# Early products without GpSimd work, and scale and shift of the second token set on the transposed tiles

## The chip, the cores and the metric

The kernel runs on one core of a Trainium2 chip. Its engines are TensorE (PE in the rows; its weight loads PEld), VectorE (DVE), ScalarE (ACT), GpSimd (POOL) and SyncE (SP), which issues nearly all DMAs. Each engine runs its own instructions strictly in the order in which the program gives them; an instruction waits for semaphores that other engines or DMAs raise. The metric is the device time of one execution in microseconds.

## The reference

Two layers of a diffusion backbone over 768 tokens (256 context, 512 latent) of width 1024. Each layer is a half-step feed-forward block, a token mixer (differential attention in layer 0, neighbourhood attention in layer 1), and a second half-step feed-forward block. Each sub-layer normalises before and after itself, and shift, scale and gate come from a conditioning vector:

```
def _rmsnorm(h, g):
    hf = hf * lax.rsqrt(jnp.mean(hf * hf, axis=-1, keepdims=True) + NORM_EPS)
    return hf.astype(h.dtype) * g

def _ffn_sublayer(h, mod, g_pre, g_post, w_in, w_out):
    shift, scale, gate = mod
    u = _rmsnorm(h, g_pre) * (1 + scale) + shift
    a, b = jnp.split(u @ w_in, 2, axis=-1)
    y = (jax.nn.silu(a) * b) @ w_out
    return h + MACARON_W * gate * _rmsnorm(y, g_post)

for i in range(2):          # mods of x from silu(c), of the context from silu(c_ctx)
    h = _ffn_sublayer(h, mods[0:3], ...)
    h = h + mods[5] * _rmsnorm(mixer(modulate(_rmsnorm(h, g[2]))), g[3])
    h = _ffn_sublayer(h, mods[6:9], ...)     # in the last layer, latent tokens only
```

In the differential attention each head's output is normalised, multiplied by a learned gain of 128 numbers (`da_subln_g`) and by a constant; the kernel folds both into one column, `gsub`.

## The kernel before

**Products.** Every fp32 operand of a matmul is split into a high part (a ScalarE cast to fp32r, `...h`) and a low part (an fp32 subtraction, `...l`), and a product is three matmul passes: hi x hi, lo x hi, hi x lo (`mm3`, line 132; the split's two instructions have lines 126 and 127).

**First gemms.** The four feed-forward blocks are `f00`, `f01` (layer 0), `f10`, `f11` (layer 1); `u @ w_in` of each is a `FirstGemm`. The six token tiles of 128 make two sets, tiles 0 to 2 and 3 to 5 (`f11`: two sets of two latent tiles, 2, 3 and 4, 5). Most of the product is done by a Strassen-like scheme that pairs the two sets (groups "R" and "F": sums of weight quarters times sums of the two sets' `u`). Before these, while the second set's `u` isn't ready, the kernel does the products that need only the first set: the heads, items "E", 7, 7, 6 and 5 of them for `f00`, `f01`, `f10`, `f11`. One E item takes two 128x1024 weight blocks (x = 0 for a, x = 1 for b), splits each (`prep`; with `EPOOL = (1, 1, 0, 1)` the low part of block x = 0 is subtracted by GpSimd in `f00`, `f01` and `f11`; names `f003s0l` = head of f00, item 3, block 0, low), does 4 x 12 matmuls (`early_a`: `e3x`, copied by ScalarE to `e3p`; `early_b`: `e3v`, to which VectorE adds `e3p`, giving `e3s`, line 533), then a SiLU on ScalarE and the product a x b on GpSimd (line 537), which goes to HBM by a DMA (`hr`). PSUM gives the `e..x` and `e..v` products a few banks in turn: a product waits until an older one has been added or copied out.

**The second set beside the heads.** A generator, stepped by `late_step()` between the head's products, makes the second set's `u`: `rest` (residual, line 905; norm), then `u_rows`: scale and shift row-wise, `un = h * rstd * A + B` with A and B as 128x1024 rows (lines 352 and 353 on VectorE; `UCOL` gives the columns of one tile that go to ScalarE and GpSimd instead, lines 347 to 349: 768 of 1024 before `f01`, all before `f10`, 384 before `f11`), then `to_sums`: eight TensorE transposes per tile into a pair of PSUM banks and, from there, eleven VectorE and five ScalarE instructions that form the sums and their splits (lines 312 to 331). In `f00` the modulation is done otherwise: by columns after the transposes (lines 189 to 193), `us` and `ut`.

**Order.** A list scheduler sets the order on each engine when the kernel is built; engines keep it. Around the `f00` head stands the load of `gsub` (line 1058) and its VectorE scaling (line 1059). The modulation rows are computed pairwise in `mods_pairs` (`mb`, `am`, lines 243 to 247), beside the first gemms.

Of the kernel before, what the change touches and what calls it, by code (L numbers as in the profile page):

```python
# [41 lines left out]
EPOOL = (1, 1, 0, 1)  # L42
UCOL = (((0, 0, 0), (0, 0, 0)), ((0, 0, 0), (0, 640, 0)), ((0, 0, 0), (0, 0, 768)), ((0, 0, 0), (0, 1024, 0)), ((0, 0, 0), (0, 640, 0)), ((0, 0, 0), (0, 384, 0)))
# [13 lines left out]
def kernel(  # L57
# [12 lines left out]
    da_subln: bass.AP,  # L70
# [63 lines left out]
    svec = const.tile([P, 5 * KC], F32, name="svec")  # L134
# [3 lines left out]
    ucol = svec[:, 2 * KC :].rearrange("p (m k o) -> p m k o", m=3, o=1)  # L138
# [160 lines left out]
    def to_sums(pool, t, first, un, ps, sums, name):  # L299
# [34 lines left out]
    def u_rows(pool, tiles, hs, uns, rows, pss, name, sums=None, rs=None, split_u=None, by_act=False):  # L334
        rs = rs or []
        n_t = len(tiles)
        for n in range(n_t + 2):
            if n < n_t and len(rs) <= n:
                rs.append(rstd_of(pool, hs[n], uns[n], f"{name}_{tiles[n]}", by_act and n == 2))
            if 0 < n <= n_t:  # L340
                un = uns[n - 1]
                k = kind(tiles[n - 1])
                a, b = rows["A", k], rows["B", k]
                cut = split_u[n - 1] if split_u else 0
                if cut:
                    c = slice(0, cut)
                    nc.scalar.activation(un[:, c], hs[n - 1][:, c], AF.Copy, scale=rs[n - 1])
                    nc.gpsimd.tensor_tensor(out=un[:, c], in0=un[:, c], in1=a[:, c], op=ALU.mult)
                    nc.gpsimd.tensor_tensor(out=un[:, c], in0=un[:, c], in1=b[:, c], op=ALU.add)
# [4 lines left out]
            yield
            if n > 1:
                t = tiles[n - 2]
                if sums:
# [60 lines left out]
    class FirstGemm:  # L418
        def __init__(self, pool, l, j, sets, name, lead=False):
# [1115 lines left out]
```

## Time and profile before

| | |
|---|---|
| time, median of 3 runs | 2891.31 us (2886.37 to 2895.78) |
| the profiled execution | 2882.43 us, span 2880.0 us, mean granted TensorE clock 0.988 |
| TensorE busy | 2755.4 us (96%) |
| VectorE, ScalarE, GpSimd busy | 1986.4 (69%), 1209.5 (42%), 883.0 us (31%) |
| heads on TensorE | f00 32.6 to 122.2 us, f01 1045.2 to 1124.4, f10 1595.7 to 1656.5, f11 2497.7 to 2547.3 |

Rows read as follows. A timeline row has start, duration, engine, line, operation, what it writes and reads with the shape, and in brackets the idle time before it and what ended it. Durations of neighbours overlap a little, since an instruction starts before the one in front has left the engine. A granted clock of 1.00 is 2.4 GHz; an average below it in a window means that part of the window ran at 1.2 GHz.

### The profile page before, as it was taken

How to read it: one execution, taken by the hardware profiler on the slowest of the kernel's cores; microseconds unless marked ns; L12 is line 12 of the kernel's file. 1: busy time of each engine (PE TensorE's matmuls, PEld its weight loads, DVE VectorE, ACT ScalarE, POOL GpSimd, SP SyncE). 2: the span in 40 equal slices, each digit the busy share in tenths (PEclk: the TensorE clock that was granted, in tenths of full speed). 3: DMA queues.
4: the chain of work that ended last, by engine and by line, in shares of the span. 5: the costliest groups of instructions: out<-in, count | busy, mean ns of one | idle time of the engine just before them, and what ended most of it. 6: DMA issues, size and time to landing. Idle time of an engine off the chain costs nothing. (4 is left out here: it accounts for less than half of the span.)

```text
span 2880.0 us, 41455 instructions
## 1 busy us (share of the span) xinstructions
PE 2755.4 (96%) x15928; PEld 2441.6 (85%) x15928; DVE 1986.4 (69%) x2554; ACT 1209.5 (42%) x1894; POOL 883.0 (31%) x715
## 2 busy tenths in 40 slices
PE   7799999999999988999999999999999999889999
PEld 5788998888888778899988888998878888789987
DVE  5677664667777696777555867674654556799965
ACT  5322333435555553233343522233444446544444
POOL 2455420020000055554210455340122110377710
PEclk9999999999999999999999999999999999999999
DMA  8577346643343476853465577436644444654375
GB/s 279 189 278 273 103 147 218 213 123 86 105 118 88 140 240 199 285 172 104 171 210 193 178 271 266 162 107 219 217 160 118 118 118 130 222 167 147 125 252 192
DMA packets 304820, 511.55 MB, mean 178 GB/s; under 512 B 17456, under 2 KB 226224, under 8 KB 297456
## 3 DMA queue, kind: packets, MB, share of 16 engines
q1 hardware_dynamic: 304336, 508.26, 53.7%
q8 instruction: 125, 2.05, 0.3%
q14 instruction: 71, 0.58, 0.1%
q10 hardware_dynamic: 288, 0.66, 0.1%
HBM read 410.15 MB, written 63.05 MB: 164 GB/s over the span
## 5 line engine op out<-in xcount | busy, mean ns | idle before, releaser
L1243 POOL TENSOR_TENSOR bias<-bp,nneg 128x128 f32<-128x128 f32 x112 | 52.3, 505 | 190.1 <-issue 99.2
L127 DVE TENSOR_TENSOR f01hl<-f01h,f01hh 128x384 fp32r<-128x384 f32 x44 | 26.4, 599 | 74.7 <-ACT f01hh L126 74.6
L127 DVE TENSOR_TENSOR f00hl<-f00h,f00hh 128x384 fp32r<-128x384 f32 x44 | 26.5, 602 | 72.9 <-ACT f00hh L126 72.8
L127 DVE TENSOR_TENSOR f10hl<-f10h,f10hh 128x384 fp32r<-128x384 f32 x44 | 26.0, 591 | 67.7 <-ACT f10hh L126 67.6
L243 PE MATMUL am<-aw,s 128*32 128x512 f32 x512 | 68.3, 606 | 4.1 <-DVE f10b0c L548 3.0
L126 ACT CAST f10hh<-f10h 128x384 fp32r<-128x384 f32 x44 | 22.7, 516 | 113.6 <-PE f10y L721 93.9
L126 ACT CAST f01hh<-f01h 128x384 fp32r<-128x384 f32 x44 | 22.7, 516 | 109.8 <-PE f01y L721 95.1
L126 ACT CAST f00hh<-f00h 128x384 fp32r<-128x384 f32 x44 | 22.7, 516 | 107.2 <-PE f00y L721 92.7
L132 PE MATMUL av<-pt,davh 128*128 128x256 f32 x224 | 44.6, 292 | 0.0
L247 DVE TENSOR_TENSOR mb<-am,mb 128x512 f32<-128x512 f32 x64 | 43.7, 683 | 0.0
L1305 PE MATMUL nav<-npt,navh 128*64 128x256 f32 (+1 forms) x320 | 39.3, 365 | 0.0
L132 PEld LDWEIGHTS av<-pt,davh 128*128 128x128 f32 x224 | 36.4, 193 | 1.3 <-ACT pt L1165 0.2
L1305 PEld LDWEIGHTS nav<-npt,navh 128*64 128x64 f32 x320 | 22.0, 136 | 12.2 <-issue 1.9
L132 PE MATMUL av<-pt,davl 128*128 128x256 f32 x112 | 31.7, 283 | 0.0
L126 ACT CAST f11hh<-f11h 128x256 fp32r<-128x256 f32 x44 | 17.7, 406 | 33.1 <-DMA f11h<-hr 22.1
L127 DVE TENSOR_TENSOR f11hl<-f11h,f11hh 128x256 fp32r<-128x256 f32 x44 | 20.2, 464 | 13.4 <-ACT f11hh L126 13.4
L243 PEld LDWEIGHTS am<-aw,s 128*32 128x32 f32 x512 | 10.1, 108 | 20.4 <-issue 10.2
L282 POOL TENSOR_SCALAR f01y0r<-f01y0s 128x1 f32<-128x1 f32 x1 | 0.2, 192 | 84.5 <-ACT f01y0j L276 84.5
L282 POOL TENSOR_SCALAR f10y0r<-f10y0s 128x1 f32<-128x1 f32 x1 | 0.2, 192 | 84.5 <-ACT f10y0j L276 84.5
L282 POOL TENSOR_SCALAR f00y0r<-f00y0s 128x1 f32<-128x1 f32 x1 | 0.2, 192 | 84.5 <-ACT f00y0j L276 84.5
L282 POOL TENSOR_SCALAR f00y3r<-f00y3s 128x1 f32<-128x1 f32 x1 | 0.2, 193 | 79.3 <-ACT f00y3j L276 79.3
L282 POOL TENSOR_SCALAR f10y3r<-f10y3s 128x1 f32<-128x1 f32 x1 | 0.2, 192 | 79.3 <-ACT f10y3j L276 79.3
(9736 smaller groups left out, 11615.4 us busy)
## 6 DMA issues: line engine op xcount, KB each, us to landing
aw<-in_ada_w SPq DMA_DIRECT2D x63, 1024.0 KB
f00r<-in_ffn_w_in SPq DMA_DIRECT2D x22, 1024.0 KB
f01r<-in_ffn_w_in SPq DMA_DIRECT2D x22, 1024.0 KB
f10r<-in_ffn_w_in SPq DMA_DIRECT2D x22, 1024.0 KB
f11r<-in_ffn_w_in SPq DMA_DIRECT2D x22, 1024.0 KB
f00o<-in_ffn_w_out SPq DMA_DIRECT2D x21, 1024.0 KB
f01o<-in_ffn_w_out SPq DMA_DIRECT2D x21, 1024.0 KB
f10o<-in_ffn_w_out SPq DMA_DIRECT2D x21, 1024.0 KB
```

The lines of the kernel that those rows point to most:

```text
L126: nc.scalar.copy(hi, src)
L127: eng.tensor_tensor(out=lo, in0=src, in1=hi.bitcast(F32), op=ALU.subtract)
L132: nc.tensor.matmul(ps, lhsT=lhs[i], rhs=rhs[j], start=first and n == 0, stop=last and n == 2)
L243: nc.tensor.matmul(ps[32 * c : 32 * c + 32], lhsT=s32[:, k], rhs=w[:, c // 2, c % 2 * 512 : c % 2 * 512 + 512], start=True, stop=True,)
L247: nc.vector.tensor_tensor(out=acc, in0=ps, in1=acc, op=ALU.add)
L282: nc.gpsimd.tensor_scalar(r, ss, 1.0, EPS, ALU.mult, ALU.add)
L1243: nc.gpsimd.tensor_tensor(out=bias[:, m, :].rearrange("p (a b) -> p a b", a=8), in0=view, in1=neg[:, m, :].rearrange("p (a b) -> p a b", a ...
L1305: nc.tensor.matmul(av[64 * i : 64 * i + 64, half * 256 + c0 : half * 256 + c0 + n], lhsT=made[u]["v"][0][:, key, vc : vc + 64], rhs=made[u ...
```

## The change

Five things. (1) `EPOOL` is gone: VectorE does every low part of the heads' weight splits (19 subtractions of 128x1024 move: 7 in `f00`, 7 in `f01`, 5 in `f11`). (2) The product a x b of each E item moves from GpSimd to VectorE (25: 7, 7, 6, 5). (3) For the second set before `f01`, `f10` and `f11` ScalarE alone writes `un = h * rstd` (128x1024), and after the eight transposes applies scale and shift in place on the PSUM banks with eight 128x128 activations per tile (3, 3 and 2 tiles: 64 instructions); scale and shift come as columns (`cols`, 128x2x8) by two DMAs of 4-byte elements per group of tokens. (4) `gsub` is a column of the constants loaded at the start and is scaled there. (5) In `mods_pairs` the bias and gain rows of a pair are loaded before its weights. The numbers of `UCOL` that concern (3) go; its two for the inputs of the mixers stay.

```diff
@@ -39,8 +39,7 @@
 PROG0 = "SF1F2b"
 PROG1 = "SF12Fb"
 SUMV = (2, 2, 2, 2)
-EPOOL = (1, 1, 0, 1)
-UCOL = (((0, 0, 0), (0, 0, 0)), ((0, 0, 0), (0, 640, 0)), ((0, 0, 0), (0, 0, 768)), ((0, 0, 0), (0, 1024, 0)), ((0, 0, 0), (0, 640, 0)), ((0, 0, 0), (0, 384, 0)))
+UCOL = {1: (0, 640, 0), 4: (0, 640, 0)}
 EVAC = "AA"
 JUNK = 1
 NEXT = (2, 4)
...
@@ -131,11 +129,12 @@
         for n, (i, j) in enumerate(PASSES):
             nc.tensor.matmul(ps, lhsT=lhs[i], rhs=rhs[j], start=first and n == 0, stop=last and n == 2)
 
-    svec = const.tile([P, 5 * KC], F32, name="svec")
+    svec = const.tile([P, 5 * KC + 1], F32, name="svec")
     nc.sync.dma_start(svec, cvec)
     nc.scalar.activation(svec[:, 0 : 2 * KC], svec[:, 0 : 2 * KC], AF.Silu)
     s2 = svec[:, 0 : 2 * KC].rearrange("p (j k) -> p j k", j=2)
-    ucol = svec[:, 2 * KC :].rearrange("p (m k o) -> p m k o", m=3, o=1)
+    ucol = svec[:, 2 * KC : 5 * KC].rearrange("p (m k o) -> p m k o", m=3, o=1)
+    gsub = svec[:, 5 * KC :]
     mcol = const.tile([P, 2, KC, 2], F32, name="mcol")
     s32 = const.tile([P, KC, 32], F32, name="s32")
     nc.vector.memset(s32, 0.0)
@@ -221,7 +220,6 @@
                 return
             pair, k = seq[q]
             nm = f"{pair[0][0]}{pair[0][1]}"
-            ws[q] = pair_loads(pool, pair, k)
             if k == 0:
                 for x, tag in (("b", "mb"), ("g", "araw")):
                     rows[x] = pool.tile([P, 512], F32, tag=tag, name=f"m{x}{nm}")
@@ -229,6 +227,7 @@
                         row = ada_b[l, m * D : (m + 1) * D] if x == "b" else norm_g[l, g_index[m]]
                         src = bass.AP(tensor=row.tensor, offset=row.offset, ap=[[512, 2], [0, 32], [1, 512]])
                         nc.sync.dma_start(rows[x][64 * a : 64 * a + 64, :], src)
+            ws[q] = pair_loads(pool, pair, k)
 
         load(0)
         yield
@@ -296,7 +295,7 @@
             nc.vector.tensor_tensor(out=ulo[cs], in0=tp, in1=uhi[cs].bitcast(F32), op=ALU.subtract)
             yield
 
-    def to_sums(pool, t, first, un, ps, sums, name):
+    def to_sums(pool, t, first, un, ps, sums, name, cols=None):
         tt, sub, add = nc.vector.tensor_tensor, ALU.subtract, ALU.add
         mine = slice(t * P, (t + 1) * P)
         twin = slice(first * P, (first + 1) * P)
@@ -305,6 +304,8 @@
         if un is not None:
             for k in range(KC):
                 nc.tensor.transpose(tp[:, k, :], un[:, k * P : (k + 1) * P], ident)
+            for k in range(KC):
+                nc.scalar.activation(tp[:, k], tp[:, k], AF.Identity, scale=cols[:, 1, k : k + 1], bias=cols[:, 0, k : k + 1])
             yield
         b12, b22 = tp[:, 0:4, :], tp[:, 4:8, :]
         ta = pool.tile([P, 2, 4, P], F32, tag="R1", name=name + "ta")
@@ -340,22 +341,27 @@
             if 0 < n <= n_t:
                 un = uns[n - 1]
                 k = kind(tiles[n - 1])
-                a, b = rows["A", k], rows["B", k]
-                cut = split_u[n - 1] if split_u else 0
-                if cut:
-                    c = slice(0, cut)
-                    nc.scalar.activation(un[:, c], hs[n - 1][:, c], AF.Copy, scale=rs[n - 1])
-                    nc.gpsimd.tensor_tensor(out=un[:, c], in0=un[:, c], in1=a[:, c], op=ALU.mult)
-                    nc.gpsimd.tensor_tensor(out=un[:, c], in0=un[:, c], in1=b[:, c], op=ALU.add)
-                if cut < D:
-                    c = slice(cut, D)
-                    nc.vector.scalar_tensor_tensor(un[:, c], hs[n - 1][:, c], rs[n - 1], a[:, c], ALU.mult, ALU.mult)
-                    nc.vector.tensor_tensor(out=un[:, c], in0=un[:, c], in1=b[:, c], op=ALU.add)
+                if "c" in rows:
+                    nc.scalar.activation(un, hs[n - 1], AF.Copy, scale=rs[n - 1])
+                else:
+                    a, b = rows["A", k], rows["B", k]
+                    cut = split_u[n - 1] if split_u else 0
+                    if cut:
+                        c = slice(0, cut)
+                        nc.scalar.activation(un[:, c], hs[n - 1][:, c], AF.Copy, scale=rs[n - 1])
+                        nc.gpsimd.tensor_tensor(out=un[:, c], in0=un[:, c], in1=a[:, c], op=ALU.mult)
+                        nc.gpsimd.tensor_tensor(out=un[:, c], in0=un[:, c], in1=b[:, c], op=ALU.add)
+                    if cut < D:
+                        c = slice(cut, D)
+                        nc.vector.scalar_tensor_tensor(un[:, c], hs[n - 1][:, c], rs[n - 1], a[:, c], ALU.mult, ALU.mult)
+                        nc.vector.tensor_tensor(out=un[:, c], in0=un[:, c], in1=b[:, c], op=ALU.add)
             yield
             if n > 1:
                 t = tiles[n - 2]
                 if sums:
-                    yield from to_sums(pool, t, t - sums["t2"] + sums["t1"], uns[n - 2], pss[n - 2], sums, f"{name}_{t}")
+                    yield from to_sums(
+                        pool, t, t - sums["t2"] + sums["t1"], uns[n - 2], pss[n - 2], sums, f"{name}_{t}", rows["c"][kind(t)]
+                    )
                 else:
                     yield from to_uT(t, uns[n - 2], pss[n - 2], f"{name}_{t}")
 
@@ -423,7 +429,6 @@
             self.n = len(sets[0]) * P
             self.slot = (2 * l + j) % 2
             early = EARLY[2 * l + j]
-            self.epool = EPOOL[2 * l + j]
             self.items = [("E", g, 0) for g in range(early)]
             for g in range(NF // 2):
                 self.items += [("R" if g < early else "F", g, x) for x in (0, 1)]
@@ -462,7 +467,7 @@
                         if x == 0:
                             o = pool.tile([P, 2, 2, KC, P], F32R, tag="T" + "hl"[g], name=f"{nm}s")
                         dst = [o[:, x, y] for y in range(2)]
-                    ops[x] = split(r[x], [P, KC, P], f"{nm}s{x}", dst, nc.gpsimd if self.epool >> x & 1 else nc.vector)
+                    ops[x] = split(r[x], [P, KC, P], f"{nm}s{x}", dst)
                     yield
                 return
             a12, a21, a22 = r[:, 4:8, 0:P], r[:, 0:4, P:256], r[:, 4:8, P:256]
@@ -534,7 +539,7 @@
                 if x == 0:
                     nc.scalar.activation(sa[0], sa[0], AF.Silu)
                     late_step()
-            nc.gpsimd.tensor_tensor(out=sa[0], in0=sa[0], in1=sa[1], op=ALU.mult)
+            nc.vector.tensor_tensor(out=sa[0], in0=sa[0], in1=sa[1], op=ALU.mult)
             nc.sync.dma_start(hdr[self.slot][2 * g][:, self.t1 * P : self.t1 * P + n], sa[0])
             self.step(i + 1, 9)
             late_step()
@@ -896,8 +901,16 @@
         rs = []
         yns = [x[0] for x in st]
         if nxt is not None:
-            rows_for(pool, nxt[0], nxt[1] + 1, kinds, "A", rows)
-            rows_for(pool, nxt[0], nxt[1], kinds, "B", rows)
+            turn = nxt[1] != 3 and si == 1
+            if turn:
+                rows["c"] = {}
+                for j in kinds:
+                    cols = rows["c"][j] = pool.tile([P, 2, KC], F32, tag=f"cols{j}", name=f"{name}c{j}")
+                    for m in range(2):
+                        nc.sync.dma_start(cols[:, m], mdram[nxt[0]][nxt[1] + m][j].rearrange("(k p) -> p k", p=P))
+            else:
+                rows_for(pool, nxt[0], nxt[1] + 1, kinds, "A", rows)
+                rows_for(pool, nxt[0], nxt[1], kinds, "B", rows)
         for n, t in enumerate(tiles):
             cut = D // 2 if nxt is None and final and n == len(tiles) - 1 else D
             for z in range(0, D, cut):
@@ -917,7 +930,7 @@
             if nxt[1] != 3 and si == 1:
                 sums = more[1] = sums_for(pool, more[0], name, 2 * nxt[0] + nxt[1] // 6)
             pss = [ys[t] for t in tiles] if final else [None] * len(tiles)
-            yield from u_rows(pool, tiles, [hs[t] for t in tiles], yns, rows, pss, name, sums, rs, UCOL[3 * nxt[0] + nxt[1] // 3][si], nxt[1] == 3 and si)
+            yield from u_rows(pool, tiles, [hs[t] for t in tiles], yns, rows, pss, name, sums, rs, UCOL.get(3 * nxt[0] + nxt[1] // 3) if si else None, nxt[1] == 3 and si)
 
     def raw_cols(w, c0, nm):
         r = wraw([P, KC, 256], nm)
@@ -1054,9 +1067,6 @@
         w = da_w_in
         cs = pool.tile([P, 2, NLAT], F32, name="rope", bufs=1)
         nc.sync.dma_start(cs, rope_cs)
-        gsub = const.tile([P, 1], F32, name="gsub")
-        nc.sync.dma_start(gsub, da_subln.rearrange("(p o) -> p o", o=1))
-        nc.vector.tensor_scalar(gsub, gsub, 1.0 - LAM_INIT, None, ALU.mult)
         lv = pool.tile([P, 4, 64], F32, tag="oo", name="lv", bufs=1)
         nc.sync.dma_start(lv, da_lambda.rearrange("a d -> (a d)").partition_broadcast(P).rearrange("p (a d) -> p a d", a=4))
         lp = pool.tile([P, 2, 64], F32, tag="sq", name="lp", bufs=1)
...
@@ -1399,6 +1409,7 @@
         first = FirstGemm(mp, 0, 0, full, "f00", lead=True)
         nc.vector.tensor_scalar(ucol[:, 1], ucol[:, 1], 1.0, None, ALU.add)
         nc.vector.tensor_tensor(out=ucol[:, 1], in0=ucol[:, 1], in1=ucol[:, 2], op=ALU.mult)
+        nc.vector.tensor_scalar(gsub, gsub, 1.0 - LAM_INIT, None, ALU.mult)
         turns = {}
         new_u("in")
 
...
```

VectorE in the `f00` head, before, around the scaling of `gsub` (`us` is tile 5 before its sums, `in_5ta` its first sum, `f004s1l` and `f005s1l` the low parts of weight blocks):

```order
L331 TENSOR_TENSOR inul<-in_4tb,inuh 128x4x128
L533 TENSOR_TENSOR f00e3s_725<-f00e3v_744,f00e3p 128x384
L127 TENSOR_TENSOR f004s1l<-f00r_570,f004s1h 128x1024
L192 TENSOR_TENSOR us_799<-in5T,mcol 128x1024
L1059 TENSOR_SCALAR gsub<-gsub 128x1
L193 TENSOR_TENSOR us_799<-us_799,mcol 128x1024
L313 TENSOR_TENSOR in_5ta<-us_799,inuh 128x512
L327 TENSOR_TENSOR inul<-us_799,inuh 128x4x128
L314 TENSOR_TENSOR in_5ta<-in_5ta,inul 128x512
L324 TENSOR_TENSOR in_5tb<-us_799,in_5tb 128x512
```

and after:

```order
L538 TENSOR_TENSOR f00e3s_726<-f00e3v_745,f00e3p 128x384
L125 TENSOR_TENSOR f004s1l<-f00r_571,f004s1h 128x1024
L542 TENSOR_TENSOR f00e3s_725<-f00e3s_725,f00e3s_726 128x384
L191 TENSOR_TENSOR us_800<-in5T,mcol 128x1024
L125 TENSOR_TENSOR f005s0l<-f00r_674,f005s0h 128x1024
L192 TENSOR_TENSOR us_800<-us_800,mcol 128x1024
L538 TENSOR_TENSOR f00e4s_828<-f00e4v_830,f00e4p 128x384
L314 TENSOR_TENSOR in_5ta<-us_800,inuh 128x512
L328 TENSOR_TENSOR inul<-us_800,inuh 128x4x128
L315 TENSOR_TENSOR in_5ta<-in_5ta,inul 128x512
```

The `gsub` instruction is gone from between the two steps of `us`; the product `f00e3s` x `f00e3s` (line 542) and `f005s0l` have come in.

VectorE at the start of the `f01` head, before (`o0i` is the residual, `o0n` its normalised and modulated rows, tiles 3 to 5 in turn):

```order
L352 SCALAR_TENSOR_TENSOR o0n_9397<-o0i_9345,o_3r,A_07_9218 128x1024
L127 TENSOR_TENSOR f011s1l<-f01r_9354,f011s1h 128x1024
L533 TENSOR_TENSOR f01e0s_9488<-f01e0v_9506,f01e0p 128x384
L353 TENSOR_TENSOR o0n_9397<-o0n_9397,B_06_9222 128x1024
L352 SCALAR_TENSOR_TENSOR o0n_9405<-o0i_9347,o_4r,A_07_9218 128x1024
L352 SCALAR_TENSOR_TENSOR o0n_9413<-o0i_9349,o_5r,A_07_9218 128x256
L353 TENSOR_TENSOR o0n_9405<-o0n_9405,B_06_9222 128x1024
L353 TENSOR_TENSOR o0n_9413<-o0n_9413,B_06_9222 128x256
L313 TENSOR_TENSOR o_3ta<-o0y_8999,o0uh 128x512
L314 TENSOR_TENSOR o_3ta<-o_3ta,o0ul 128x512
L533 TENSOR_TENSOR f01e1s_9585<-f01e1v_9587,f01e1p 128x384
L315 TENSOR_TENSOR o_3ta<-o0y_8999,o_3ta 128x512
```

and after:

```order
L125 TENSOR_TENSOR f011s0l<-f01r_9352,f011s0h 128x1024
L538 TENSOR_TENSOR f01e0s_9488<-f01e0v_9490,f01e0p 128x384
L538 TENSOR_TENSOR f01e0s_9489<-f01e0v_9507,f01e0p 128x384
L125 TENSOR_TENSOR f011s1l<-f01r_9352,f011s1h 128x1024
L542 TENSOR_TENSOR f01e0s_9488<-f01e0s_9488,f01e0s_9489 128x384
L125 TENSOR_TENSOR f012s0l<-f01r_9447,f012s0h 128x1024
L538 TENSOR_TENSOR f01e1s_9592<-f01e1v_9594,f01e1p 128x384
L125 TENSOR_TENSOR f012s1l<-f01r_9447,f012s1h 128x1024
L538 TENSOR_TENSOR f01e1s_9593<-f01e1v_9616,f01e1p 128x384
L542 TENSOR_TENSOR f01e1s_9592<-f01e1s_9592,f01e1s_9593 128x384
L125 TENSOR_TENSOR f013s0l<-f01r_9533,f013s0h 128x1024
L314 TENSOR_TENSOR o_3ta<-o0y_8997,o0uh 128x512
```

The row-wise steps of lines 352 and 353 are gone from in front of the first addition of `f01e1s`; low parts `...s0l` and products of line 542 have come in, and the sums of tile 3 stand behind item 1.

ScalarE at the same place, before:

```order
L126 CAST f012s0h<-f01r_9446 128x1024
L519 COPY f01e1p<-f01e1x_9537 128x384
L347 ACTIVATE o0n_9413<-o0i_9349,o_5r 128x768
L519 COPY f01e1p<-f01e1x_9538 128x384
L312 CAST o0uh<-o0y_8999 128x4x128
L126 CAST f012s1h<-f01r_9446 128x1024
```

and after:

```order
L124 CAST f012s0h<-f01r_9447 128x1024
L308 ACTIVATE o0y_8997<-o0y_8997,o0c_9437 128x128
L345 ACTIVATE o0n_9411<-o0i_9347,o_5r 128x1024
L308 ACTIVATE o0y_8997<-o0y_8997,o0c_9437 128x128
L124 CAST f012s1h<-f01r_9447 128x1024
L308 ACTIVATE o0y_8997<-o0y_8997,o0c_9437 128x128
L540 ACTIVATE f01e1s_9592<-f01e1s_9592 128x384
L308 ACTIVATE o0y_8997<-o0y_8997,o0c_9437 128x128
L124 CAST f013s0h<-f01r_9533 128x1024
L308 ACTIVATE o0y_8997<-o0y_8997,o0c_9437 128x128 x3
L524 COPY f01e2p<-f01e2x_9647 128x384
L308 ACTIVATE o0y_8997<-o0y_8997,o0c_9437 128x128
L313 CAST o0uh<-o0y_8997 128x4x128
```

In front of the first cast of tile 3's sums (line 313; line 312 before) there now stand that tile's eight in-place activations (line 308), and among them a whole-row copy of another tile (line 345), three weight casts, a SiLU and a copy of item 2.

## Rows read from the trace of the kernel before

**Rows 1.** The page, part 1: busy time, share of the span and instructions of each engine.

```profile
PE 2755.4 (96%) x15928; PEld 2441.6 (85%) x15928; DVE 1986.4 (69%) x2554; ACT 1209.5 (42%) x1894; POOL 883.0 (31%) x715
```

**Rows 2.** The waits of TensorE: who, for what; us in total, times, longest.

```profile
PE f01e2x L132 <- DVE f01e1s L533: 5.5, 1, 5.5
PE f00e4v L132 <- ACT f00e4p L519: 5.3, 1, 5.3
PE f01b0W L132 <- DVE mb L247: 5.1, 1, 5.1
PE f11a0X L132 <- ACT f115bh L126: 4.8, 1, 4.8
...
PE f01e5x L132 <- DVE f01e4s L533: 3.7, 2, 3.3
...
PE f00e5x L132 <- ACT f00e5p L519: 3.0, 1, 3.0
...
PE f11e2x L132 <- DVE f11e1s L533: 2.9, 1, 2.9
...
PE f00e4x L132 <- DVE f00e3s L533: 2.6, 1, 2.6
...
PE f00b0W L132 <- DVE mb L247: 2.2, 1, 2.2
```

**Rows 3.** Windows: length, busy (instructions) of each engine, granted clock, DMA share, GB/s.

```profile
53.00:123.00 70.00, 55.88 (x289) 53.32 (x288) 54.66 (x56) 32.15 (x49) 31.98 (x21) 0.90 0.58 179
93.00:110.00 17.00, 12.62 (x39) 11.64 (x40) 15.90 (x14) 6.99 (x12) 11.37 (x6) 0.62 0.32 109
1045.00:1125.00 80.00, 68.14 (x367) 64.81 (x366) 68.78 (x65) 41.42 (x64) 49.32 (x33) 0.94 0.64 199
1595.00:1657.00 62.00, 56.81 (x321) 53.52 (x320) 58.38 (x63) 35.66 (x57) 30.32 (x22) 1.00 0.60 194
2497.00:2548.00 51.00, 37.77 (x266) 35.42 (x267) 46.36 (x46) 27.14 (x45) 32.47 (x22) 0.90 0.56 179
```

**Rows 4.** Timeline of VectorE, 88 to 96 us: start, us, line, operation [idle before].

```profile
91.38 0.15 DVE L1059 TENSOR_SCALAR gsub<-gsub 128x1 f32<-128x1 f32 x1 [5.98 <-DMA gsub<-in_da_subln]
...
93.35 0.69 DVE L327 TENSOR_TENSOR inul<-us,inuh 128x512 fp32r<-128x512 f32 x1
```

**Rows 5.** Timeline of ScalarE, 88 to 96 us.

```profile
92.70 0.62 ACT L312 CAST inuh<-us 128x512 fp32r<-128x512 f32 x1 [9.44 <-DVE us L193]
```

**Rows 6.** Timeline of SyncE's queue, 78 to 92 us.

```profile
80.31 1.09 SPq L1058 DMA_DIRECT2D gsub<-in_da_subln  x1
```

**Rows 7.** Timeline of GpSimd, 53 to 60 us.

```profile
56.43 2.67 POOL L127 TENSOR_TENSOR f003s0l<-f00r,f003s0h 128x1024 fp32r<-128x1024 f32 x1
```

**Rows 8.** Timeline of VectorE, 53 to 123 us.

```profile
57.15 2.50 DVE L327 TENSOR_TENSOR inul<-us,inuh 128x512 fp32r<-128x512 f32 x1 [0.31 <-ACT inuh L312]
...
114.87 1.84 DVE L127 TENSOR_TENSOR f007bl<-f007s,f007bh 128x1024 fp32r<-128x1024 f32 x1 [0.39 <-ACT f007bh L126]
```

**Rows 9.** Timeline of VectorE, 1045 to 1125 us.

```profile
1047.09 3.32 DVE L905 SCALAR_TENSOR_TENSOR o0i<-o0n,o0y3r,o0i 128x1024 f32<-128x1024 f32 x1
...
1063.62 4.78 DVE L353 TENSOR_TENSOR o0n<-o0n,B 128x1024 f32<-128x1024 f32 x2
...
1069.64 0.55 DVE L533 TENSOR_TENSOR f01e1s<-f01e1v,f01e1p 128x384 f32<-128x384 f32 x1
...
1108.35 2.40 DVE L127 TENSOR_TENSOR f017dl<-f01r,f017dh 128x512 fp32r<-128x512 f32 x1
```

**Rows 10.** Groups by line and form, VectorE, 53 to 123 us: busy, mean ns.

```profile
L127 DVE TENSOR_TENSOR f003s1l<-f00r,f003s1h 128x1024 fp32r<-128x1024 f32 x1 | 1.2, 1218 | 0.0
```

**Rows 11.** One line's instructions: ns shortest/median/longest, from and to, shape.

```profile
L537 POOL TENSOR_TENSOR f00e0s<-f00e0s,f00e0s x1: 1007/1007/1007, 52.6 to 52.6; 128x384 f32<-128x384 f32 x1
```

**Rows 12.** The same of another line, on ScalarE.

```profile
L189 ACT ACTIVATE ut<-in2T,mcol x8: 449/458/475, 28.0 to 43.3; 128x128 f32<-128x128 f32 x8
```

**Rows 13.** The same of a third line, on ScalarE.

```profile
L347 ACT ACTIVATE f01n<-f01i,f_4r x1: 1158/1158/1158, 1603.3 to 1603.3; 128x1024 f32<-128x1024 f32 x1
```

More of the change, by code (lines that the diff above doesn't have):

```diff
@@ L69 @@
     da_lambda: bass.AP,
-    da_subln: bass.AP,
     na_w_in: bass.AP,
@@ L1328 @@
         OVER = {
-            "post": (("h", 3), ("yn", 3), ("G0", 1), ("A0", 1), ("B0", 1), ("R1", 2), ("ss", 4), ("rs", 4)),
+            "post": (("h", 3), ("yn", 3), ("G0", 1), ("A0", 1), ("B0", 1), ("R1", 2), ("ss", 4), ("rs", 4), ("cols0", 1)),
             "mid": (("sa", 2), ("c0", 1), ("c1", 1), ("u2", 2), ("aw", 2), ("mb", 2)),
@@ L1487 @@
             np.asarray(a).reshape(-1, P).T
-            for a in (inputs["c"], inputs["c_ctx"], inputs["ada_b"][0, : 2 * D], inputs["norm_g"][0, 0])
+            for a in (inputs["c"], inputs["c_ctx"], inputs["ada_b"][0, : 2 * D], inputs["norm_g"][0, 0], inputs["da_subln_g"][0])
         ],
@@ L1520 @@
         "da_w_in": inputs["da_w_in"][0], "da_w_out": inputs["da_w_out"][0], "da_lambda": inputs["da_lambda"][0],
-        "da_subln": inputs["da_subln_g"][0], "na_w_in": inputs["na_w_in"][0], "na_w_out": inputs["na_w_out"][0],
+        "na_w_in": inputs["na_w_in"][0], "na_w_out": inputs["na_w_out"][0],
         "rpb_pad": runs, "rope_cs": rope, "na_neg": neg,
```

## The prediction

> **What bounds the kernel now.** I read the page's busy shares first: TensorE is busy for 96% of the span [rows 1], so a change to the other engines counts only where TensorE waits for them or runs at a lower clock. The view of TensorE's waits says where [rows 2]: nearly all of its long waits for VectorE and ScalarE lie in the heads (names `e2x`, `e4v`, `e5x`, `a0X`), besides two on the modulation sums (`mb`). The windows give each head a ceiling [rows 3]: TensorE idles 14.1 us of 70 in the later part of the `f00` head (70 less 55.88 busy), 11.9 of 80 in `f01`, 5.2 of 62 in `f10`, 13.2 of 51 in `f11`. There is a second loss: the granted clock is 0.90, 0.94, 1.00 and 0.90, and just 0.62 from 93 to 110 us, behind the 5.3 us wait of `f00e4v`. A mean of 0.62 between the levels 1.2 and 2.4 GHz is 76% of the time at the lower one; 76% of the 12.62 busy us, halved, is 4.8 us lost. VectorE is the fullest of the others there (54.7 of 70, 68.8 of 80, 58.4 of 62, 46.4 of 51).
>
> Two things fill it. One is a stall: VectorE sat 5.98 us at 91.38 for the DMA of `gsub`, which nothing in the head needs, between two steps of tile 5's `us` [rows 4]; ScalarE, in order, stood 9.44 us at the cast of `us` with the copy `f00e4p` behind it [rows 5], and TensorE waited 5.3 us for that copy [rows 2]. The other is a stretch: a subtraction of 128x512 takes 0.69 us [rows 4], but 2.50 at 57.15 [rows 8], inside GpSimd's `f003s0l` (56.43, 2.67 us) [rows 7]. Against the usual duration of their shape, 12 VectorE instructions of the `f00` head (the first at 57.15, the last at 114.87 [rows 8]) are too long by 13.9 us in sum, 15 in the `f01` head (1047.09 to 1108.35 [rows 9]) by 19.3.
>
> **The change part by part.**
> *Work onto VectorE.* A 128x1024 subtraction takes 1.22 us [rows 10], a 128x384 operation 0.55 [rows 9]; less some 0.08 that neighbours overlap, 1.14 and 0.47. `f00` and `f01` get 7 x (1.14 + 0.47) = 11.3 us each, `f10` 6 x 0.47 = 2.8, `f11` 5 x 1.14 and 5 products of two thirds the size, some 7.3. The product itself isn't shown on VectorE; its ends are the addition of the same size (0.55) and GpSimd's 1.01 [rows 11]; I take 0.55, VectorE's own.
>
> *f00.* Freed: 6.0 (`gsub`) + 13.9 (stretch, as GpSimd has no work of size left in the head) - 11.3 = 8.6 us by which VectorE is ahead when it reaches `f005s1l`, for which item 5 waits. Half of the clock's 4.8 comes back, 2.4. The low parts of items 1 and 2 now stand in front of the first set's `inul`, which delays the first products: -1.5 (between 0 and two subtractions, 2.4). Sum +9.5. What is late next is VectorE still, not TensorE.
>
> *f01.* The row-wise steps go: 2.25 tiles of two instructions near 1.2 us, 5.2; their stretch is inside the 19.3 (the pair at 1063.62 took 4.78 [rows 9]). 5.2 + 19.3 - 11.3 = 13.2 us. The first addition of `f01e1s` at 1069.64 [rows 9], for which TensorE waited 5.5 [rows 2], then follows its product at once. But sums now come in whole blocks: tile 3's, eleven instructions of some 0.6 us, stand in front of `f013s1l`, and cannot begin before ScalarE has done three casts and eight activations. From the order and these durations I get waits of some 2.8 us for two of the tiles: 13.2 - 5.6 = +7.6, within the ceiling of 11.9 idle and some 4 of clock.
>
> *f10.* The freed time exceeds what TensorE loses (5.2 idle, clock 1.00 [rows 3]); half of it: +2.6 (0 to 5).
>
> *f11.* Waits of 2.9 (`f11e2x`) and 4.8 (`f11a0X`) hang on the same two causes [rows 2]; with a clock of 0.90 I take +6 (2 to 9); behind the head the groups wait for VectorE anyhow.
>
> *In-place scale and shift.* 64 activations of 128x128. The nearest row is the same operation from PSUM into SBUF, 458 ns [rows 12]; into PSUM it isn't shown. Ends: 128x512 in one cast took 0.62 [rows 5], so 155 ns of pure data each, and 475, the longest [rows 12]. At 458 it is 3.7 us per tile, 29.3 in all, and eight copies of 1.16 [rows 13] less the three that were partly there, some 6 more. ScalarE is busy 41.4 of 80 us, 35.7 of 62 and 27.1 of 51 [rows 3], so 11 to 13 us per head find room: I price them at nothing beyond the 5.6 taken off above. If the room is no cover, they cost up to 35.
>
> *Columns.* Six DMAs in place of the second set's rows. Nearest row: `gsub`, also of 4-byte elements, held SyncE's queue for 1.09 us [rows 6] and its reader stood until 11.1 us after the issue [rows 4, 6]. They are issued among the head's weight loads, well over 11 us before the first activation: 0, at most 6 x 1.09 = 6.5 if the weight loads behind them come late by it.
> The Trainium skill (DMA: Bandwidth & Descriptors, Specifications) puts the smallest transfer at line rate at 512 bytes and says that smaller ones are done as read-modify-write; it speaks against these columns. The 11.1 us of `gsub` agree, though they hold the queue's wait too. By the rule the columns would be priced at their upper end, 6.5, and the forecast would come to 2869.5.
>
> *gsub and the modulation rows.* With its load at the start, `gsub` costs one small VectorE instruction there: 0. The two waits for `mb` (5.1 and 2.2 [rows 2]) came from a low part in front of it on VectorE that waits for a late load; in the new order it stands further behind. A third of 7.3: +2.5 (-1 to 6).
>
> Sum: 9.5 + 7.6 + 2.6 + 6 + 2.5 = 28.2. From the profiled execution's 2882.4 this makes 2854.2. That execution was 8.9 below the median of the runs shown (2891.3); on the median, 2863.
>
> **The stretch, weighed.** All rests on the stretch being GpSimd's doing; what the rows show is overlap in time. The Trainium skill (GPSIMD Engine Reference, Key points) says that GpSimd shares its SBUF interfaces with VectorE, and that instructions with two SBUF inputs contend. By that rule the 33 us go with the moved work; without it they stay, which is the second rival below.
>
> **Rivals.**
> 1. *ScalarE becomes the bound (slower).* In each of the three heads its activations stand among the weight casts and the copies that free PSUM banks. From the point at which its queue is later than TensorE's next product, every added instruction is exposed: 29.3 + 6 = 35.3 against 28.2 gained is +7, and a lower clock behind such waits some 3 more: 2901. Against it: half of ScalarE's time in `f01` is free; for it: it runs in order, and it stood 9.44 us once already. 6%.
> 2. *The stretch stays.* Then `f00` gets 6.0 - 11.3, `f01` 5.2 - 11.3, `f11` 3.9 (1.6 tiles' row-wise steps at 2.4) - 7.3, `f10` 4.8 (two tiles') - 2.8, the modulation 2.5: -10.3, so 2902. Against it: long instructions begin and end with GpSimd's. 4%.
> 3. *Loads and stores pace the heads.* Then only the gsub stall goes: 6.0, 2885. For it: each item needs 1 MB of weights, and a DMA share of 0.64 [rows 3]; against it: TensorE's longest waits there name VectorE and ScalarE. 11%.
> 4. *TensorE runs through.* The waits of all heads go (44.4 us idle in rows 3), about what they hold less the transposes' own gaps: some 42, 2849. It needs a VectorE with room, which the sums above don't leave in `f00`. 8%.
>
> **How the numbers follow.** The forecast, 2863, has 71%, with 2849 to 2878 as its own range from the terms' ends. Rivals 1 and 2 have 10%, 3 has 11%, 4 has 8%. About 0.3% (8.7 us) is what a measurement of this kernel tells from no change: faster is under 2882.6, so 0.71 + 0.08 = 0.79; same 0.11; slower 0.10. The range from 2843 to 2886 takes in rivals 3 and 4 and leaves out the slower ones and a gain above 48.
>
> **What would show it.** Right: no VectorE idle for a DMA near 80 to 92 us, `f00e4v` waiting under 1 us, and a clock near 1.00 where it was 0.62; 128x512 subtractions in the heads at 0.7 us; `f01e2x` waiting under 1 us and waits of 2 to 3 us at `f01e3x` or `f01e4x`; activations of line 308 near 0.46 us. Wrong: ScalarE's activations ending TensorE's waits (rival 1), long VectorE instructions with GpSimd idle (rival 2), DMA as the releaser of head items (rival 3), or VectorE waiting for `cols`.

## The result, and the profile after

The changed kernel takes 2861.0 us (median of 4, 2858.8 to 2862.2) against 2890.1 of the kernel before on the same chip: a ratio of 0.9897, interval 0.9879 to 0.9915, so 25 to 35 us less. The forecast was 2863. Between the two profiled executions the spans differ by less, 2880.0 to 2859.1: that of before was one of its fastest (2882.4, where its median over 17 runs is 2889.9), that of after stands at its median. What follows by stages adds up to these 20.9 us.

The page's busy shares after answer to [rows 1]: GpSimd is 100 us less busy, and VectorE 33, though it took over GpSimd's work in the heads.

```profile
PE 2749.9 (96%) x15928; PEld 2438.5 (85%) x15928; DVE 1953.7 (68%) x2584; ACT 1237.4 (43%) x1963; POOL 783.3 (27%) x665
```

TensorE's waits after, to be read beside [rows 2] (who, for what; us in total, times, longest):

```profile
PE f00e4v L130 <- DVE f00e3s L538: 6.2, 1, 6.2
PE f01e3x L130 <- DVE f01e2s L538: 5.5, 1, 5.5
...
PE f00e5x L130 <- ACT f00e5p L524: 3.9, 1, 3.9
...
PE f11e3x L130 <- ACT f11e3p L524: 3.0, 1, 3.0
PE f01e5x L130 <- DVE f01e4s L538: 3.0, 1, 3.0
...
PE f10e4v L130 <- DVE f10e3s L538: 2.0, 1, 2.0
```

Gone are the waits for `mb` at `f01b0W` and `f00b0W` (5.1 and 2.2) and that of `f11a0X`; that of `f01e2x` has shrunk to 0.9. But `f00e4v` waits longer than before, and a wait of 5.5 us has come at `f01e3x`, both now for an addition of VectorE. VectorE's timelines at the two places show what that addition waited for:

```profile
68.95 0.69 DVE L328 TENSOR_TENSOR inul<-us,inuh 128x512 fp32r<-128x512 f32 x1
...
75.90 0.69 DVE L332 TENSOR_TENSOR inul<-in_4tb,inuh 128x512 fp32r<-128x512 f32 x1
83.30 0.56 DVE L538 TENSOR_TENSOR f00e3s<-f00e3v,f00e3p 128x384 f32<-128x384 f32 x1 [6.72 <-DMA hr<-f00e2s]
```

```profile
1068.35 0.69 DVE L332 TENSOR_TENSOR o0ul<-o_3tb,o0uh 128x512 fp32r<-128x512 f32 x1
1074.92 0.56 DVE L538 TENSOR_TENSOR f01e2s<-f01e2v,f01e2p 128x384 f32<-128x384 f32 x1 [5.89 <-DMA hr<-f01e1s]
```

The 128x512 subtraction has its 0.69 us ([rows 8]: 2.50), and GpSimd is idle. The stall of 5.98 us for `gsub` [rows 4] is gone, and one of 6.72 stands in its place: the addition writes a buffer that the store of the item before (`hr<-f00e2s`) has not yet left. SyncE's queue tells why:

```profile
61.36 3.46 SPq L229 DMA_DIRECT2D mg<-in_norm_g  x4
64.92 10.62 SPq L451 DMA_DIRECT2D f00r<-in_ffn_w_in  x2
75.64 3.72 SPq L543 DMA_DIRECT2D hr<-f00e2s  x1
```

Behind six loads of gain rows (`mg`, 128 KB each, of which these are the last four) two weight loads hold the queue for 10.62 us instead of some 0.5 each, and the store, ready at 68.4 when VectorE's product ended, gets through only then, from 75.64. The DMA view of 62 to 84 us has the other half (40 slices; busy share of the 16 DMA engines in tenths, and GB/s):

```profile
DMA  9411111111111116997211121179971159931100
GB/s 413 186 48 48 52 48 48 54 48 50 52 52 48 52 58 209 276 313 168 53 45 52 48 78 52 62 240 301 279 154 46 41 195 397 393 113 47 56 22 11
```

From 63 to 70 us only one to two tenths of the engines are busy, at 48 to 54 GB/s. By heads the windows answer to [rows 3] (length, busy of PE, PEld, DVE, ACT, POOL, clock, DMA share, GB/s):

```profile
51.00:116.00 65.00, 53.77 (x290) 51.97 (x289) 51.34 (x65) 30.17 (x47) 10.61 (x8) 0.89 0.53 167
1038.00:1117.00 79.00, 66.88 (x368) 64.56 (x368) 57.30 (x71) 51.05 (x89) 14.29 (x17) 0.94 0.61 193
1583.00:1642.00 59.00, 55.54 (x315) 54.21 (x314) 49.53 (x62) 46.15 (x81) 16.17 (x14) 0.97 0.64 209
2479.00:2524.00 45.00, 36.72 (x261) 34.35 (x262) 37.36 (x48) 32.23 (x59) 11.26 (x11) 0.92 0.62 195
```

VectorE is now busy for 57.3 of 79 us in `f01` (68.8 of 80), ScalarE for 51.1 (41.4). From the first to the last product of each head on TensorE's timeline, and of the groups of `f00`, `f01` and `f10` together (the paired products behind each head), in us:

| profiled execution | f00 head | f01 head | f10 head | f11 head | groups |
|---|---|---|---|---|---|
| before | 89.6 | 79.2 | 60.8 | 49.6 | 889.5 |
| after | 84.8 | 78.1 | 58.9 | 44.5 | 882.2 |
| e5 (rows cut, changed kernel) | 77.3 | 72.3 | 57.8 | 44.8 | 874.5 |
| e7 (idle GpSimd work, changed kernel) | 90.2 | 82.5 | 57.8 | 47.8 | 881.2 |
| e9 (rows cut, kernel before) | 83.1 | 77.2 | 60.8 | 49.5 | 873.3 |
| e10 (parts 3 to 5 alone) | 82.4 | 88.3 | 57.7 | 42.5 | 890.6 |

### The profile page after: what moved, and what is told of

It is laid out like the page before. It is cut to its first block, busy times and chain, and to the rows that moved or that the text cites. A ratio compares the mean times of both kernels' runs of the same rounds, so it can differ in the third digit from the quotient of the medians.

```text
span 2859.1 us, 41468 instructions
## 1 busy us (share of the span) xinstructions
PE 2749.9 (96%) x15928; PEld 2438.5 (85%) x15928; DVE 1953.7 (68%) x2584; ACT 1237.4 (43%) x1963; POOL 783.3 (27%) x665
## 5 line engine op out<-in xcount | busy, mean ns | idle before, releaser
L242 PEld LDWEIGHTS am<-aw,s 128*32 128x32 f32 x512 | 10.3, 107 | 20.8 <-issue 10.3
```

The lines of the kernel that those rows point to most:

```text
L242: nc.tensor.matmul(ps[32 * c : 32 * c + 32], lhsT=s32[:, k], rhs=w[:, c // 2, c % 2 * 512 : c % 2 * 512 + 512], start=True, stop=True,)
```

## The experiments

Times are medians; each ratio is to the kernel before, run on the same chip (2889.3 to 2889.9 there). The list scheduler orders every variant anew, so a run differs from its neighbour by more than the lines of its diff.

**e1, part 5 undone.** `ws[q] = pair_loads(...)` goes back ahead of the rows' loads.

> The changed kernel with part 5 alone undone (a pair's weights are loaded ahead of its rows again). Theory A, SyncE's queue: the rows loaded ahead of the weights stand in the queue right in front of the stores that VectorE waits for in the f00 and f01 heads (6.7 and 5.9 us); undone, those two waits fall under 3 us each and the time goes from 2861 to about 2854. Theory B, the stores are late whatever the order of the rows: the waits stay and the time is within 3 us of 2861. Theory C, part 5 is what took the 5.1 us wait on the modulation sums away behind the f01 head: the wait comes back and the time is about 2865.

2859.2 us, 0.9897 (0.9884 to 0.9911): the same as the changed kernel. Both waits stayed (6.8 and 6.0 us on VectorE) and the wait on the sums did not come back, so A and C fall and B holds: whichever way a pair's loads are written, the scheduler puts the rows in front of the store.

**e2, part 4 alone.**

```diff
-    svec = const.tile([P, 5 * KC], F32, name="svec")
+    svec = const.tile([P, 5 * KC + 1], F32, name="svec")
+    gsub = svec[:, 5 * KC :]
-        nc.sync.dma_start(gsub, da_subln.rearrange("(p o) -> p o", o=1))
```

> The kernel before with part 4 alone (gsub loaded and scaled at the start). Theory A, the 6.0 us stall of VectorE is the cause of the longest f00 wait and of the low clock behind it: 6 to 9 us less, about 2882. Theory B, the store of the item before (hr from f00e2s) or the stretch is next and takes its place: 0 to 3 us less, 2887 to 2890.

2883.6 us, 0.9980 (0.9971 to 0.9989): 5.8 us less (3 to 8). A. In its trace part of the gain is lost behind the head, where VectorE's sum for `mb` is waited for longer than in [rows 2]:

```profile
PE f00b0W L131 <- DVE mb L247: 5.6, 1, 5.6
```

**e3, parts 1 and 2 alone.**

```diff
-  ops[x] = split(r[x], [P, KC, P], f"{nm}s{x}", dst, nc.gpsimd if self.epool >> x & 1 else nc.vector)
+  ops[x] = split(r[x], [P, KC, P], f"{nm}s{x}", dst)
-  nc.gpsimd.tensor_tensor(out=sa[0], in0=sa[0], in1=sa[1], op=ALU.mult)
+  nc.vector.tensor_tensor(out=sa[0], in0=sa[0], in1=sa[1], op=ALU.mult)
```

> The kernel before with parts 1 and 2 alone (low parts and products of the heads on VectorE, nothing else). Theory A, the stretch is GpSimd's doing: VectorE gains 33 us of stretch in the f00 and f01 heads for 22.6 us of added work, 8 to 14 us less in all, about 2879. Theory B, the stretch stays or was hidden: the added work shows, 5 to 15 us more, about 2899.

2876.5 us, 0.9956 (0.9942 to 0.9969): 12.7 us less (9 to 17). A: more work on VectorE made the kernel faster. But the 12.7 us aren't the price of the stretch by itself. In its trace the scaling of `gsub` stands at 109.7 us, so that the stall of [rows 4] is gone without part 4, and VectorE already waits 7.2 and 9.3 us for the stores `hr<-f00e2s` and `hr<-f01e1s`.

**e4, part 3 alone** (the hunks of `to_sums`, `u_rows` and `rest`).

```diff
+            for k in range(KC):
+                nc.scalar.activation(tp[:, k], tp[:, k], AF.Identity, scale=cols[:, 1, k : k + 1], bias=cols[:, 0, k : k + 1])
```

> The kernel before with part 3 alone (scale and shift of the second token set in place by ScalarE). Theory A, VectorE and GpSimd are relieved in the f01, f10 and f11 heads and ScalarE has room: 6 to 12 us less, about 2881. Theory B, ScalarE becomes the bound in these heads: no gain or up to 10 us more, 2890 to 2900.

2882.4 us, 0.9975 (0.9965 to 0.9985): 7.2 us less (4 to 10). A in sum, not in each head: in its profile `f11`'s head fell to 41.5 us, but `f01`'s rose to 82.4, with ScalarE's `f01e4p` ending a wait of 3.3.

**e5, the rows cut.**

```diff
-  src = bass.AP(tensor=row.tensor, offset=row.offset, ap=[[512, 2], [0, 32], [1, 512]])
-  nc.sync.dma_start(rows[x][64 * a : 64 * a + 64, :], src)
+  for h in range(2):
+      src = bass.AP(tensor=row.tensor, offset=row.offset + 512 * h, ap=[[0, 32], [1, 512]])
+      nc.sync.dma_start(rows[x][64 * a + 32 * h : 64 * a + 32 * h + 32, :], src)
```

> The changed kernel with each DMA of a 64-partition bias or gain row cut into two of 32 partitions. Theory A: these rows move at some 50 GB/s with about an eighth of the DMA engines busy, because one such DMA is shared out by its outermost dimension of two; the loads and stores behind them in SyncE's queue stand for that, and VectorE waits 6.7 and 5.9 us for the stores of e2s (f00) and e1s (f01). Cut, the rows go out over more engines, both waits fall under 1 us and the time to about 2850 (2846 to 2855). Theory B, the rows are slow for another reason (all partitions read one address), or the store is late on its own account: the share stays at an eighth, the waits stay, 2858 to 2864.

2839.4 us, 0.9824 (0.9811 to 0.9838): 22 us under the changed kernel, and under A's range. The same queue and the same DMA view:

```profile
65.80 1.02 SPq L452 DMA_DIRECT2D f00r<-in_ffn_w_in  x2
69.60 0.34 SPq L544 DMA_DIRECT2D hr<-f00e2s  x1
```

```profile
DMA  0299540006999999929986610100000004679998
GB/s 25 110 397 298 201 164 26 0 21 186 288 328 333 315 298 296 266 41 397 330 153 216 175 52 0 30 0 0 0 0 0 0 0 45 140 235 328 382 298 290
```

The two weight loads hold the queue for 1.02 us, the store for 0.34, six tenths or more of the engines are busy in most slices from 67 to 75 us, and VectorE waits for no store. TensorE's longest waits in the heads are now for VectorE's last low part of item 5:

```profile
PE f01e5x L130 <- DVE f015s1l L125: 5.1, 1, 5.1
PE f00e5x L130 <- DVE f005s1l L125: 4.8, 1, 4.8
```

**e6, the store on ScalarE's queue.**

```diff
-  nc.sync.dma_start(hdr[self.slot][2 * g][:, self.t1 * P : self.t1 * P + n], sa[0])
+  nc.scalar.dma_start(hdr[self.slot][2 * g][:, self.t1 * P : self.t1 * P + n], sa[0])
```

> The changed kernel with the store of a head's product issued from ScalarE's queue, not SyncE's. Theory A, the store is late only since it stands behind blocked loads in SyncE's queue: VectorE's waits for the two stores go, 2850 to 2855. Theory B, ScalarE, which must wait for VectorE's product before it can issue, holds up its own copies behind it: the waits turn up at TensorE's products with ScalarE as releaser, 2860 or more.

2854.8 us, 0.9883 (0.9867 to 0.9898): 6 us less by the medians, 4 by the ratios, whose intervals overlap; that it is faster isn't shown. Something of both: the waits for the two stores went, others came (`f11e3v` 5.6 and `f01e2v` 3.4 us for ScalarE's copies, and VectorE 3.4 and 3.0 for two other stores, those of `f01e4s` and `f00e0s`).

**e7, idle work on GpSimd.** The result of the added subtraction is read by nothing.

```diff
   ops[x] = split(r[x], [P, KC, P], f"{nm}s{x}", dst)
+  if x == 0 and self.nm != "f10":
+      nc.gpsimd.tensor_tensor(out=r[x], in0=r[x], in1=ops[x][0].bitcast(F32), op=ALU.subtract)
```

> The changed kernel with an idle subtraction of 128x1024 on GpSimd in each head item of f00, f01 and f11 but the first, in place on the raw weights, whose result nothing reads: GpSimd is busy as before the change, VectorE's work is that of the changed kernel. Theory A, the stretch is GpSimd's doing: VectorE's subtractions and sums beside it take 1.5 to 3 us again, some 15 to 25 us of stretch return in the heads and the time rises by 8 to 20 us, to 2869 to 2881. Theory B, the stretch had another cause: VectorE's instructions keep their 0.7 and 1.2 us, 2859 to 2864.

2873.2 us, 0.9942 (0.9929 to 0.9956): 12 us more than the changed kernel. A. GpSimd's and VectorE's timelines:

```profile
58.49 3.20 POOL L472 TENSOR_TENSOR f00r<-f00r,f003s0h 128x1024 f32<-128x1024 f32 x1
```

```profile
59.55 0.56 DVE L540 TENSOR_TENSOR f00e1s<-f00e1v,f00e1p 128x384 f32<-128x384 f32 x1
60.02 2.22 DVE L314 TENSOR_TENSOR in_3ta<-us,inuh 128x512 f32<-128x512 f32 x1
...
63.23 0.68 DVE L325 TENSOR_TENSOR in_3tb<-us,in_3tb 128x512 f32<-128x512 f32 x1
```

```profile
110.13 2.40 POOL L472 TENSOR_TENSOR f00r<-f00r,f006s0h 128x1024 f32<-128x1024 f32 x1 [7.43 <-DVE f006s0l L125]
```

```profile
110.39 3.21 DVE L125 TENSOR_TENSOR f006s1l<-f00r,f006s1h 128x1024 fp32r<-128x1024 f32 x1
113.53 0.68 DVE L125 TENSOR_TENSOR f007dl<-f00r,f007dh 128x512 fp32r<-128x512 f32 x1
```

The sum at 60.02 takes 2.22 us beside GpSimd's subtraction and its like at 63.23, behind it, 0.68; the low part at 110.39 takes 3.21 instead of 1.22. From 53 us on the stretch in the `f00` head is 10.3 us over 8 instructions, in `f01` 13.1 over 10 (changed kernel: 4.6 over 5, 3.3 over 4); by the table the heads with the added work take 3.3 to 5.4 us longer, and `f10`, without it, doesn't.

**e8, part 4 undone.** The diff of e2 turned round, on the changed kernel.

> The changed kernel with part 4 alone undone (gsub loaded and scaled in the f00 head again). Theory A, part 4 is worth the same as alone, about 6 us: 2867. Theory B, in the changed kernel VectorE stands in the same place for a store anyway, so that the two waits lie over each other: 2861 to 2864. Theory C, they add up and the clock falls further: 2869 or more.

2858.3 us, 0.9892 (0.9879 to 0.9906): part 4 is worth nothing in the changed kernel. The time is B's, or a little under it, but B's reason is wrong: VectorE doesn't wait for `gsub` at all. The scheduler put its scaling behind item 5, where the load had long landed:

```profile
107.70 0.14 DVE L1072 TENSOR_SCALAR gsub<-gsub 128x1 f32<-128x1 f32 x1
```

**e9, the rows cut in the kernel before** (the diff of e5).

> The kernel before with each bias or gain row's DMA cut into two of 32 partitions, as in e5, and nothing else. Theory A, the slow rows cost the kernel before little, since its heads were late through the gsub stall and the stretch and its stores were waited for by only 1 to 2 us: 0 to 6 us less, 2884 to 2889; the change made them the next bound. Theory B, they cost it as much as the changed kernel: about 22 us less, 2867.

2862.9 us, 0.9909 (0.9894 to 0.9924): 26 us less (22 to 31), with none of the change's five parts. B, and against my reading: the slow rows were not uncovered by the change, they had cost the kernel before as much. By the table 16.2 us are gained in the groups, where the waits of 5.1 and 2.2 us for `mb` are gone, and 6.5 and 2.0 in the `f00` and `f01` heads (some 5 are lost elsewhere; the two profiles differ by 19.2). `gsub` is issued in less than half the time of [rows 6]; VectorE doesn't wait for it, though in this order its scaling comes only at 100.6 us. The clock of the later `f00` head is 0.98 ([rows 3]: 0.90):

```profile
89.87 0.43 SPq L1059 DMA_DIRECT2D gsub<-in_da_subln  x1
```

```profile
53.00:123.00 70.00, 59.23 (x331) 57.14 (x332) 54.38 (x60) 35.08 (x52) 40.25 (x25) 0.98 0.63 197
```

**e10, parts 1 and 2 undone** (the diff of e3 turned round, on the changed kernel).

> The changed kernel with parts 1 and 2 undone (heads' first low parts and products on GpSimd again), parts 3 to 5 kept. Theory A, the parts add up: 13 us more than the changed kernel, as much as parts 1 and 2 gave alone, 2873. Theory B, they need each other: relieved of the row-wise steps VectorE and GpSimd have room, so that less than 8 us are lost, under 2868; or the stretch bites more, over 2878.

2882.0 us, 0.9977 (0.9969 to 0.9986): 21 us more than the changed kernel, beyond A and in the upper part of B. Parts 1 and 2 are worth 13 alone and 21 beside the others. Not all of that is stretch: against the changed kernel's profile the `f00` head is 2.4 us shorter, the groups take 8.4 more, with a wait for `mb` in them again, and the `f01` head takes 88.3 us, 9 more than before, with ScalarE among its releasers:

```profile
PE f00b0W L131 <- DVE mb L247: 6.6, 1, 6.6
...
PE f01e6x L131 <- DVE f01e5s L540: 3.4, 1, 3.4
PE f01e4v L131 <- ACT f01e4p L526: 3.3, 1, 3.3
...
PE f01e1x L131 <- ACT f01e0s L542: 2.5, 1, 2.5
```

**e11, e5 with part 2 undone; e12, e5 with two low parts on GpSimd.**

```diff
-  nc.vector.tensor_tensor(out=sa[0], in0=sa[0], in1=sa[1], op=ALU.mult)                  # e11
+  nc.gpsimd.tensor_tensor(out=sa[0], in0=sa[0], in1=sa[1], op=ALU.mult)
-  ops[x] = split(r[x], [P, KC, P], f"{nm}s{x}", dst)                                     # e12
+  ops[x] = split(..., dst, nc.gpsimd if x == 1 and i == 5 and self.nm in ("f00", "f01") else nc.vector)
```

> e5 with part 2 undone (the product a x b of a head item on GpSimd again). Theory A, VectorE is the bound of the heads in e5 (TensorE waits 4.8 and 5.1 us for the low parts f005s1l and f015s1l), and 0.47 us per item less on it is worth more than the stretch that 1 us of GpSimd per item brings: 2835 to 2838. Theory B, the stretch takes more than the product frees, as in part 1: 2841 to 2846.

> e5 with the second low part of item 5 of the f00 and f01 heads on GpSimd (two subtractions of 128x1024). Theory A, they are what TensorE waits for longest in e5 (4.8 and 5.1 us), standing on VectorE behind tile 5's sums; GpSimd, idle, has them done sooner: 5 to 8 us less than e5, 2831 to 2835. Theory B, the sums beside it stretch and the additions behind them come as late: 2838 to 2841.

e11: 2838.3 us, 0.9825 (0.9811 to 0.9840): no difference from e5 that can be told; part 2 by itself is worth nothing there. e12: 2836.6 us, 0.9820 (0.9806 to 0.9834), the lowest median, but its interval and e5's overlap nearly wholly: inconclusive. Both beat the kernel before and the changed one. The wait for `f005s1l` went and one of 4.7 us for ScalarE's `f00e5p` stands at the same product.

## Why the prediction was right, and where it was wrong

- **The total** came out (28.2 us forecast, 25 to 35 measured), but not by its terms. Between the two profiles, which the terms were made from, the change is 20.9 us: 4.8 + 1.1 + 1.9 + 5.1 in the four heads, 7.3 in the groups, and 0.7 for the rest (1.5 each gained before the `f00` and `f11` heads, 2.4 lost behind `f11`'s). The medians are 8 us further apart than the profiles. So the near hit is luck in part: terms of 28.2 us stand against 20.9, and the difference came from what the other executions of the kernel before lost. Their mean granted clock goes along with it (0.988 in the profiled one; 0.984 to 0.986 in most of the others, which took 2886 to 2894 us); where in the kernel they lost it, its one trace doesn't show.
- **The stretch is GpSimd's doing**: right, shown by e7 from the other side: GpSimd's work alone brings long instructions back, and 12 us with them. Of 33.2 us in `f00` and `f01` 25.3 went; what is left begins where GpSimd forms the first group's weight sums, which the change leaves there. The second rival falls.
- **f00, +9.5, was 4.8.** The failing step is "what is late next is VectorE still". Next was a store: `f00e4v` waits 6.2 us for an addition that waits 6.72 for `hr<-f00e2s`. With the rows cut (e5) the head loses another 7.5 us. The 2.4 us for the clock didn't come either: over the later head it stays at 0.89 ([rows 3]: 0.90), since a new wait stands in place of the old; in e5, without it, the window from 51 to 110 us has 0.97.
- **f01, +7.6, was 1.1**, for the same reason. Two waits of 2.8 us behind blocks of sums were forecast; there is one of 5.5 at `f01e3x`, and the sums' block had ended (1069.0) when VectorE still waited, to 1074.92, for `hr<-f01e1s`. Rival 3, at 11%, had loads and stores pace the heads and left the change no gain but that of `gsub`. Its mechanism was there, beside gains of other parts, so that the total hid it.
- **f10, +2.6, and f11, +6**, were 1.9 and 5.1: right in size.
- **In-place activations**: right. They take 0.43 us (0.458 taken), and nothing waits for the columns' DMAs, issued 20 us ahead:

```profile
L308 ACT ACTIVATE o0y<-o0y,o0c x24: 409/434/458, 1053.8 to 1086.2; 128x128 f32<-128x128 f32 x24
```

```profile
L910 SPq DMA_DIRECT2D o0c<-md x2: 1248/1958/2667, 1032.0 to 1033.3; - x2
```

  Rival 1 is not what decides here, but e4 and e10 show its beginning: with GpSimd still in the heads the in-place steps lengthen `f01`'s by 3 and 9 us.
- **gsub** was sized right alone (5.8 us for 6.0), but not as a term of a sum: e8 has it at nothing, since the order that comes with parts 1 and 2 moves its scaling out of the way by itself (e3: 109.7 us, e8: 107.70). I read 11.1 us from its issue to its use as the price of 4-byte elements, and said that the Trainium skill's rule (DMA: Bandwidth & Descriptors, Specifications) on transfers under 512 bytes agreed. The trace of the kernel before doesn't bear that out: between 82.0 and 83.2 us 126 packets under 512 bytes pass, nearly all of the load's 128 elements, at most 3 us after the issue. Packets of 2 KB, the size of the gain rows' pieces, run on until 90.6, and VectorE starts at 91.38. So it had waited for the gain rows in front of it in the queue. The columns, together sixteen times as many elements, are waited for by nobody.
- **The modulation rows**, +2.5, were worth more: TensorE's waits for `mb` in the groups fall from 7.5 us in all to 2.6, which is 4.9 of the 7.3 us of the groups. e1 shows that part 5 was not the cause, and the other traces show no single part that was: part 3 alone (e4) leaves waits of 3.2 and 1.6 us, parts 1 and 2 alone (e3) leave 6.2 at `f01b0W` and bring 6.7 at `f10b0W`. With the rows cut (e5, e9) there is none.

## What to carry to other kernels

When a stall is taken out, look along the same engine's row of waits for what it would have met next, and follow that one through the DMA queue as well: here a stall on a load and one on a store had the same cause, a few slow broadcast rows at the head of the queue, and repairing that alone was worth about as much as the whole change (26 and 29 us). A busy share of one tenth in the DMA view, while an issue that usually takes half a microsecond takes five or ten, is the sign. An engine's relief by a helper that reads the same memory is to be counted net of the stretch: taking GpSimd's help in the heads away was worth 13 us alone and 21 beside the other parts, though stalls on stores and on `mb` moved with it both times; with the rows cut, giving it the products back (e11) changed nothing.

## What the runs showed of the hardware

A DMA of one row into 64 partitions, written as two halves of 32 repeats, moved about 50 GB/s with one to two tenths of the DMA engines busy. Written as two DMAs of 32 repeats the same rows, alone in e5's view from 64.2 to 65.3 us, moved 201 and 164 GB/s with five and four tenths busy, and the queue behind them was free. That the outermost dimension of two decides how many engines take part fits this, but the other explanations were not each tried.

VectorE's long instructions beside GpSimd were those with both operands in SBUF. In the `f01` head of the kernel before two operations with one operand in PSUM fall inside GpSimd's instructions and keep their time (0.67 and 0.54 us); the next one, with both in SBUF, takes 1.45 instead of 0.69:

```profile
1102.07 2.24 POOL L474 TENSOR_TENSOR f017s<-f017s,f01r 128x512 f32<-128x512 f32 x1
1104.38 1.29 POOL L476 TENSOR_TENSOR f017s<-f01r,f017s 128x512 f32<-128x512 f32 x1
```

```profile
1103.71 0.67 DVE L327 TENSOR_TENSOR o0ul<-o0y,o0uh 128x512 fp32r<-128x512 f32 x1
1104.30 0.54 DVE L533 TENSOR_TENSOR f01e4s<-f01e4v,f01e4p 128x384 f32<-128x384 f32 x1
1104.77 1.45 DVE L329 TENSOR_TENSOR o0Tl<-o_5tb,o0Th 128x512 fp32r<-128x512 f32 x1
```

The long ones look like waits rather than half speed: they end about their usual time after GpSimd's instruction does (128x512: 59.65 after 59.10 [rows 7, 8], and in e7 62.24 after 61.69; 128x1024, in e7: 113.60 after 112.53).
